# Grouped attention on one core: loads in order of need, a TensorE kept awake at the start, correction chains of eight with one step on GpSimd

## The chip, the cores and the metric

The kernel runs on one core of a Trainium2 chip. The metric is the device time of one execution in microseconds (us). Every time below is the median of a kernel's runs. In the profile PE is TensorE (its matmuls), PEld its weight loads, ACT ScalarE, DVE VectorE, POOL GpSimd, and SP or SPq is SyncE.

## The reference

```python
# q: 8 x 8 x 1024 x 64 (batch, query heads, sequence, head size); k, v: 8 x 2 x 1024 x 64; float32
scale = 1.0 / np.sqrt(head_dim)
for g in range(n_kv_heads):              # four query heads share one K and one V
    scores = scale * np.matmul(q_group, k_group.transpose(0, 1, 3, 2))
    attn = np.exp(scores - np.max(scores, axis=-1, keepdims=True))
    attn = attn / (np.sum(attn, axis=-1, keepdims=True) + 1e-08)
    output[:, q_start:q_end] = np.matmul(attn, v_group)
```

That is 64 heads. The kernel splits a head into two jobs of 512 queries and a job into eight blocks of 128 keys, so there are 128 jobs and 1024 blocks of scores of 128x512.

## The kernel before

Each block of scores needs an exponential, and two engines make them. ScalarE takes two blocks at a time from PSUM (128x1024). VectorE takes single blocks: it writes the bits of an approximate power of two, gathers four such blocks into a group, and corrects the group by a chain of four steps: an AND, a linear factor, a product, and an addition to the bits. (The plan and the prediction count the last two alike, as products: both are operations of two inputs, and they take the same time.) A plan, made before the launch from assumed durations, decides which block goes to which engine, and places every instruction in a fixed order.

```python
GROUP = 4
# in the plan: all four steps of a chain are VectorE's
CHAIN = (0.73, 0.73, 1.26, 1.26)
...
# one cursor `nxt` walks through all blocks; each goes to the engine that is free first
ta, td = ...            # when ScalarE's, when VectorE's PSUM bank is free
t, to_d = (ta, 0) if ta <= td else (td, 1)
```

Inputs are loaded in three stages. GpSimd issues a transfer that casts a head to bf16 into scratch memory; SyncE issues transfers that transpose it into SBUF, 256 rows at a time; K's parts are then placed into a padded set by four more transfers that GpSimd issues. SyncE also issues the 128 outputs.

```python
PIECE = 256
def cast(key, src):
    dma = nc.gpsimd.dma_start(out=scr..., in_=src...)
    tc.add_manual_dep(dma.ins, last_score[0].name, SYNC, reason="pace")   # not before this score
def transpose(key, dst, n):
    rows = slice(n * PIECE, (n + 1) * PIECE)
    nc.sync.dma_start_transpose(out=dst[:, rows], in_=src[rows, :])
def place_k(b, g, side, parity):
    nc.gpsimd.dma_start(out=ksets[b % 2][...], in_=kT[(b, g)][...])
...
elif step == 1:                                   # the linear factor
    nc.vector.tensor_scalar(out=y, in0=z, scalar1=CURVE_A / 128.0, scalar2=CURVE_B,
                            op0=ALU.mult, op1=ALU.add)
elif step == 2:
    nc.vector.tensor_tensor(out=y, in0=z, in1=y, op=ALU.mult)
...
def normalise(s):                                 # output bank -> SBUF -> memory
    nc.vector.reciprocal(out=rec, in_=o[:, :, D])
    nc.vector.tensor_tensor(out=ost, in0=o[:, :, 0:D], in1=rec..., op=ALU.mult)
    nc.sync.dma_start(out=out[b, h]..., in_=ost)
...
# when the loads stand in the queues, relative to a head's first score at th (plan time)
at(th - 28.0, cast, ("q", b, h), q[b, h])
at(th - 17.0 + n, transpose_q, b, h, n)           # n = 0, 1
at(th - 38.0, cast, ("k", b, g), k[b, g])
at(th - 27.0 + n, transpose_k, b, g, n)
at(th - 20.0, place_k, b, g, side, parity)        # four of them
```

Every engine works through its instructions in the order in which they were placed. This order is what the change edits.

The softmax here doesn't subtract the row's maximum and nothing guards it: scores larger than these inputs give would overflow.

Of the kernel before, what the change touches and what calls it, by code (L numbers as in the profile page):

```python
# [14 lines left out]
GROUP = 4  # L15


def make_plan(nj, nkc):
# [6 lines left out]
    QK, PV, EXP, P1, NORM = 0.214, 0.143, 0.925, 0.605, 0.57  # L25
    CHAIN = (0.73, 0.73, 1.26, 1.26)
    FROM_PE, FROM_ACT, FROM_DVE = 0.28, 0.18, 0.12
    LIVE_A, LIVE_D, PENDING, ONLY_A = 26, 6, 8, 14
    INF = 1e9
    n = nj * nkc  # L30
# [3 lines left out]
    nxt = 0  # L34
    open_jobs, next_job, rem, obank = [], 0, {}, {}
    open_a = None
# [5 lines left out]

    def first_free(slots):
        return min(range(len(slots)), key=lambda s: slots[s])

    while normed < nj:
        best = None
        if nxt < n:
            ta = td = INF
            if open_a is not None:  # L50
                ta = max(pe, open_a["t"])
            elif live["A"] < LIVE_A:
                ta = max(pe, min(a_free))
            if pending < PENDING and nxt < n - ONLY_A and (cur or live["D"] < LIVE_D):
                td = max(pe, min(bank))
            t, to_d = (ta, 0) if ta <= td else (td, 1)
            if t < INF:
                best = min(best or (INF,), (t, 1 + to_d, "qk", to_d))
        for i, s in enumerate(open_jobs):
            for c in rem[s]:  # L60
                at = max(pe, ready.get(s * nkc + c, INF))
                if at < INF:
                    best = min(best or (INF,), (at, 3 + i, "pv", (s, c)))
        if len(open_jobs) < 2 and next_job < nj:
            at = max(pe, min(obank_free), min(ready.get(next_job * nkc + c, INF) for c in range(nkc)))
            if at < INF:
                best = min(best or (INF,), (at, 3 + len(open_jobs), "open", next_job))
        for q, p, kind in ((normq, 0, "norm"), (p1q, 1, "p1"), (chainq, 2, "chain")):
            if q:
                best = min(best or (INF,), (max(dve, q[0][0]), p, kind, 0))  # L70
        if cur and nxt >= n - ONLY_A and not p1q:
            best = min(best or (INF,), (dve, 9, "flush", 0))
        t, _, kind, arg = best
        if kind == "qk":
            cell = nxt
            nxt += 1
            pe = t + QK
            if not arg:
                if open_a is None:
                    slot = first_free(a_free)  # L80
                    a_id += 1
                    live["A"] += 1
                    open_a = {"slot": slot, "t": a_free[slot], "cells": []}
                    a_free[slot] = INF
                o = open_a
                ops.append((t, "qk", cell, "A", a_id, o["slot"], len(o["cells"])))
                o["cells"].append(cell)
                home[cell] = ("A", a_id)
                if len(o["cells"]) == 2 or nxt >= n:
                    act = max(act, pe + FROM_PE)  # L90
                    ops.append((act, "exp", a_id, tuple(o["cells"])))
                    act += EXP * len(o["cells"]) / 2
                    a_free[o["slot"]] = act + FROM_ACT
                    uses[("A", a_id)] = len(o["cells"])
                    for x in o["cells"]:
                        ready[x] = act + FROM_ACT
                    open_a = None
            else:
                k = first_free(bank)
                bank[k] = INF  # L100
                pending += 1
                ops.append((t, "qk", cell, "D", k, 0, 0))
                p1q.append((pe + FROM_PE, cell, k))
# [28 lines left out]
        elif kind == "p1":  # L132
            _, cell, k = p1q.pop(0)
            if not cur:
                d_id += 1
                live["D"] += 1
            ops.append((t, "p1", cell, k, d_id, len(cur)))
            dve = t + P1
            bank[k] = dve + FROM_DVE
            cur.append(cell)  # L140
            home[cell] = ("D", d_id)
            if len(cur) == GROUP:
                chainq.append((dve, d_id, cur, 0))
                cur = []
        elif kind == "flush":
            chainq.append((dve, d_id, cur, 0))
            cur = []
        else:
            _, g, cells, step = chainq.pop(0)
            ops.append((t, "chain", g, len(cells), step))  # L150
            dve = t + CHAIN[step] * len(cells) / GROUP
            if step + 1 < len(CHAIN):
                chainq.insert(0, (dve, g, cells, step + 1))
            else:
                pending -= len(cells)
                uses[("D", g)] = len(cells)
                for x in cells:
                    ready[x] = dve + FROM_DVE
# [4 lines left out]
def kernel(  # L163
# [27 lines left out]
    PIECE = 256  # L191
    scale = 1.0 / math.sqrt(D)
# [15 lines left out]
    qT_pool = ctx.enter_context(tc.tile_pool(name="qTpool", bufs=8))  # L208
    kT_pool = ctx.enter_context(tc.tile_pool(name="kTpool", bufs=4))
    pa_pool = ctx.enter_context(tc.tile_pool(name="papool", bufs=26))  # L210
    pd_pool = ctx.enter_context(tc.tile_pool(name="pdpool", bufs=6))
# [13 lines left out]

    ident = const_pool.tile([128, 128], BF16)
    make_identity(nc, ident)
    vsets, ksets = [], []
    for s in range(2):
# [4 lines left out]
        for side in range(2):  # L234
            if s == 0:
                nc.vector.memset(ks[(1 - side) * D : (2 - side) * D, :, side, :], 0.0)
# [52 lines left out]
    def first_loads():  # L289

        staged = []
        for eng, src in ((nc.sync, k[0, 0]), (nc.scalar, q[0, 0])):
            f = first_pool.tile([128, NHC, 2, D], FP32, name=f"f{len(staged)}")
            eng.dma_start(
                out=f, in_=src.rearrange("(c p two) d -> p c two d", p=128, two=2)
            )
            staged.append(f)
        vf = first_pool.tile([128, NHC, 2, D], FP32, name="vf")
        nc.sync.dma_start(
            out=vf, in_=v[0, 0].rearrange("(c p two) d -> p c two d", p=128, two=2)  # L300
        )
        cast(("q", 0, 1), q[0, 1])
# [5 lines left out]
        for side in range(2):  # L308
            nc.gpsimd.memset(ksets[1][(1 - side) * D : (2 - side) * D, :, side, :], 0.0)  # L309
        fk, fq = staged  # L310

        hk = first_pool.tile([128, NHC, 3, D], BF16, name="hk")
        nc.vector.tensor_copy(out=hk[:, :, 0:2, :], in_=fk)  # L313
        nc.vector.tensor_copy(out=hk[:, :, 2, :], in_=fk[:, :, 0, :])
        hq = first_pool.tile([128, NHC, 2 * D], BF16, name="hq")
        nc.scalar.copy(out=hq, in_=fq.rearrange("p c two d -> p c (two d)"))
        tk = dbanks[0].tile([128, 2, HALF], BF16, name="dps0")
        tq = dbanks[1].tile([128, HALF], BF16, name="dps1")
        for w in range(2):
            for c in range(NHC):  # L320
                nc.tensor.transpose(  # L321
                    tk[:, w, c * 128 : (c + 1) * 128],
                    hk[:, c, w : w + 2, :].rearrange("p w d -> p (w d)"),
                    ident,
                )
        for c in range(NHC):
            nc.tensor.transpose(tq[:, c * 128 : (c + 1) * 128], hq[:, c, :], ident)
        qT[(0, 0)] = qT_pool.tile([128, HALF], BF16, name="qT")
        lo, hi = slice(0, D), slice(D, 2 * D)
        nc.vector.tensor_copy(out=ksets[0][lo, 0, 0, 0:HALF], in_=tk[lo, 0, :])  # L330
        nc.scalar.copy(out=qT[(0, 0)], in_=tq)
        nc.vector.tensor_copy(out=ksets[0][lo, 0, 0, HALF:S], in_=tk[lo, 1, :])
        nc.vector.tensor_copy(out=ksets[0][hi, 0, 1, 0:HALF], in_=tk[hi, 1, :])
        nc.vector.tensor_copy(out=ksets[0][hi, 0, 1, HALF:S], in_=tk[hi, 0, :])
# [46 lines left out]
    def exp_curve(g, m, step):  # L381
# [7 lines left out]
        elif step == 1:  # L389
            y = tmp_pool.tile([128, GROUP, QBS], FP16, name="y")[:, 0:m]  # L390
            temps[g].append(y)
            nc.vector.tensor_scalar(  # L392
# [56 lines left out]
    for op in plan:  # L449
        if op[1] == "qk":  # L450
            first_use.setdefault(op[2] // NKC, op[0])
        at(op[0], run[op[1]], *op[2:])
    for b in range(B):
        for h in range(H):
            if b == 0 and h == 0:
                continue
            th = first_use[(b * H + h) * 2]
            if (b, h) != (0, 1):
                at(th - 28.0, cast, ("q", b, h), q[b, h])
            for n in range(HALF // PIECE):  # L460
                at(th - 17.0 + n, transpose_q, b, h, n)
            if h % HPG == 0:
                g = h // HPG
                at(th - 38.0, cast, ("k", b, g), k[b, g])
                at(th - 33.0, cast, ("v", b, g), v[b, g])
                for n in range(HALF // PIECE):
                    at(th - 27.0 + n, transpose_k, b, g, n)
                for side in range(2):
                    for parity in range(2):
                        at(th - 20.0, place_k, b, g, side, parity)  # L470
                at(th - 15.0, place_v, b, g)
# [34 lines left out]
```

## Time and profile before

| | before |
|---|---|
| time, median of 3 runs | 397.44 us (397.31 to 398.06) |
| span of the profiled run | 395.58 us |
| first exponential starts | 8.16 us |
| exponentials on ScalarE | 412, busy 379.0 us |
| ScalarE idle between the first and the last | 1.05 us |
| end of the last to the end of the span | 7.38 us |
| VectorE busy; GpSimd busy | 375.8 us; 86.6 us |

The main views are shown in the prediction. The page cuts the span into 40 slices and gives each engine's busy tenths in each; these are ScalarE's and GpSimd's rows for the kernel before:

```profile
ACT  4999999999999999999999999999999999999992
POOL 5340303132041313113131040312214131120000
```

A 9 means 90% or more of the slice. ScalarE has no gap that shows at this scale, and GpSimd is mostly idle.

### The profile page before, as it was taken

The numbers are of one execution on the slowest core, as the hardware profiler recorded it, in microseconds if no ns is written. First come the engines' busy times: TensorE is split into PE (matmuls) and PEld (weight loads), VectorE is DVE, ScalarE is ACT, GpSimd is POOL, SyncE is SP. The second block draws the span as 40 slices with busy tenths as digits, with TensorE's granted clock in tenths as the row PEclk, the third lists the DMA queues.
The fourth block names the chain that finished last, engine by engine and source line by source line (L and its number), as shares of the span: only waits on it lengthen the run. The fifth ranks groups of instructions, "written<-read, shape, count | busy, mean of one in ns | idle before, by whom it ended". The sixth has DMA issues, their size and how long they took to land.

```text
span 395.6 us, 12683 instructions
## 1 busy us (share of the span) xinstructions
PE 365.7 (92%) x5043; PEld 233.0 (59%) x5132; DVE 375.8 (95%) x664; ACT 381.5 (96%) x415; POOL 86.6 (22%) x165
## 2 busy tenths in 40 slices
PE   4899999999999999999999999999999999999986
PEld 2455566565656556655656565565655666565655
DVE  4999999999999999999999999999999999999995
ACT  4999999999999999999999999999999999999992
POOL 5340303132041313113131040312214131120000
PEclk9999999999999999999999999999999999999999
DMA  4665866749676786847758686785965867574314
GB/s 106 106 125 111 163 107 127 128 86 160 103 139 130 132 143 101 142 90 145 115 103 141 111 141 112 118 143 98 155 109 115 149 132 121 99 130 99 68 28 94
DMA packets 134890, 46.72 MB, mean 118 GB/s; under 512 B 130848, under 2 KB 132384, under 8 KB 133344
## 3 DMA queue, kind: packets, MB, share of 16 engines
q1 hardware_dynamic: 129408, 29.52, 38.3%
q0 software_dynamic: 4896, 16.13, 27.0%
q8 instruction: 40, 0.66, 0.8%
q10 hardware_dynamic: 528, 0.26, 0.2%
q14 instruction: 18, 0.15, 0.2%
HBM read 27.13 MB, written 28.97 MB: 142 GB/s over the span
## 4 chain that ended last, share of the span: by engine, by line
ACT 67%; DVE 11%; PE 10%; issue 6%; DMA 3%; POOL 1%; SPq 0%
ACT pa L362 67%; PE ops L414 5%; PE aps L351 5%; DVE pd L371 3%; DVE y L402 2%; DVE pd L406 2%; DVE ost L429 1%; DMA vf<-in_v_dram 1%; PE dps L351 1%; DVE y L392 1%; DMA qT<-scr_q 1%; POOL kset L309 1%; DVE z L386 1%; DVE rec L427 1%; DMA scr_q<-in_q_dram 1%
## 5 line engine op out<-in xcount | busy, mean ns | idle before, releaser
L362 ACT ACTIVATE pa<-aps 128x1024 bf16<-128x1024 f32 x412 | 379.0, 1064 | 2.1 <-PE aps L351 1.3
L351 PE MATMUL aps<-qT,kset 128*128 128x512 bf16 x735 | 226.2, 379 | 15.5 <-ACT pa L362 13.6
L414 PEld LDWEIGHTS <-pa 128*128 128x128 bf16 x3296 | 134.5, 97 | 57.6 <-DVE ost L429 0.8
L414 PE MATMUL ops<-vset,pa 128*128 128x65 bf16 x3296 | 143.9, 193 | 3.4
L371 DVE TENSOR_SCALAR pd<-dps 128x512 uint16<-128x512 f32 x200 | 129.8, 682 | 2.2 <-PE dps L351 2.2
L351 PEld LDWEIGHTS <-kset 128*128 128x128 bf16 x1024 | 85.3, 97 | 66.3 <-issue 30.9
L248 POOL DMA_DIRECT2D scr_q<-in_q_dram x63 | 34.0, 540 | 173.4 <-PE aps L351 150.6
L351 PE MATMUL dps<-qT,kset 128*128 128x512 bf16 x200 | 64.5, 380 | 1.0
L406 DVE TENSOR_TENSOR pd<-pd,y 128x2048 uint16<-128x2048 uint16 x50 | 61.2, 1225 | 1.7
L402 DVE TENSOR_TENSOR y<-z,y 128x2048 f16<-128x2048 uint16 x50 | 61.2, 1225 | 1.7
L429 DVE TENSOR_TENSOR ost<-ops,rec 128x256 f32<-128x256 f32 x128 | 54.3, 425 | 4.4
L414 PEld LDWEIGHTS <-pd 128*128 128x128 bf16 x800 | 38.5, 97 | 29.8 <-DVE pd L406 7.9
L268 POOL DMA_DIRECT2D kset<-kT x60 | 32.2, 545 | 76.7 <-DMA kT<-scr_k 68.7
L414 PE MATMUL ops<-vset,pd 128*128 128x65 bf16 x800 | 45.3, 194 | 1.2
L392 DVE TENSOR_SCALAR y<-z 128x2048 f16<-128x2048 uint16 x50 | 34.3, 687 | 0.6
L386 DVE TENSOR_SCALAR z<-pd 128x2048 uint16<-128x2048 uint16 x50 | 34.2, 684 | 0.0
L427 DVE RECIPROCAL rec<-ops 128x4 f32<-128x4 f32 x128 | 22.6, 176 | 2.4 <-PE ops L414 1.9
L248 POOL DMA_DIRECT2D scr_v<-in_v_dram x15 | 7.6, 505 | 8.2 <-PE aps L351 7.1
L248 POOL DMA_DIRECT2D scr_k<-in_k_dram x15 | 8.1, 542 | 4.7 <-PE aps L351 4.3
L321 PE MATMUL dps<-ident,hk 128*128 128x128 bf16 x8 | 1.0, 311 | 5.0 <-DVE hk L313 5.0
L321 PEld LDWEIGHTS <-hk 128*128 128x128 bf16 x8 | 0.8, 141 | 5.0 <-DVE hk L313 5.0
L309 POOL MEMSET kset<- 64x2048 bf16 x2 | 3.6, 1798 | 0.1
(20 smaller groups left out, 9.7 us busy)
## 6 DMA issues: line engine op xcount, KB each, us to landing
out_dram<-ost SPq DMA_DIRECT2D x128, 128.0 KB, 3.2
scr_q<-in_q_dram POOLq DMA_DIRECT2D x63, 128.0 KB, 3.5
kset<-kT POOLq DMA_DIRECT2D x60, 64.0 KB, 2.7
qT<-scr_q SPq DMA_TRANSPOSE x126, 3.6
scr_k<-in_k_dram POOLq DMA_DIRECT2D x15, 128.0 KB, 4.2
scr_v<-in_v_dram POOLq DMA_DIRECT2D x15, 128.0 KB, 3.9
vset<-scr_v SPq DMA_DIRECT2D x30, 64.0 KB, 3.8
kT<-scr_k SPq DMA_TRANSPOSE x30, 3.4
```

The lines of the kernel that those rows point to most:

```text
L248: dma = nc.gpsimd.dma_start(out=scr.rearrange("(p f) -> p f", f=1024), in_=src.rearrange("(p s) d -> p (s d)", s=1024 // D),)
L268: nc.gpsimd.dma_start(out=ksets[b % 2][side * D : (side + 1) * D, g, side, parity * HALF : (parity + 1) * HALF], in_=kT[(b, g)][parity * D ...
L351: last_score[0] = nc.tensor.matmul(dst, lhsT=ksets[b % 2][:, h // HPG, side, c * 128 : (c + 1) * 128], rhs=qT[(b, h)], start=True, stop=Tr ...
L362: nc.scalar.activation(out=pt[:, 0:m], in_=psum.pop(("A", n))[:, 0:m], func=AF.Exp, scale=scale)
L371: nc.vector.tensor_scalar(out=groups[g][:, slot], in0=psum.pop(cell), scalar1=bits_scale, scalar2=bits_bias, op0=ALU.mult, op1=ALU.add,)
L386: nc.vector.tensor_scalar(out=z, in0=pd, scalar1=0x7F, scalar2=None, op0=ALU.bitwise_and)
L392: nc.vector.tensor_scalar(out=y, in0=temps[g][0], scalar1=CURVE_A / 128.0, scalar2=CURVE_B, op0=ALU.mult, op1=ALU.add,)
L402: nc.vector.tensor_tensor(out=y, in0=z, in1=y, op=ALU.mult)
L406: nc.vector.tensor_tensor(out=pd, in0=pd, in1=y, op=ALU.add)
L414: nc.tensor.matmul(ops_of[s][:, qs, :], lhsT=p_of[cell][:, qs * 128 : (qs + 1) * 128], rhs=vsets[b % 2][:, h // HPG, c, :], start=opens an ...
L427: nc.vector.reciprocal(out=rec, in_=o[:, :, D])
L429: nc.vector.tensor_tensor(out=ost, in0=o[:, :, 0:D], in1=rec.unsqueeze(2).to_broadcast([128, NQS, D]), op=ALU.mult,)
```

## The change

The intent has three parts. The linear factor of the chain goes to GpSimd, which has time to spare, and groups grow from four blocks to eight, so that fixed costs per instruction fall and VectorE gets slack. The plan lets VectorE work up to six jobs ahead of ScalarE, so that its blocks are ready early; the loads are issued by when they are needed, tighter at the start and wider later. At the start, Q and K are loaded in halves and TensorE runs blank products to leave its slow clock.

```diff
-GROUP = 4
+GROUP = 8
+POOL_STEP = 1
...
-    CHAIN = (0.73, 0.73, 1.26, 1.26)
-    LIVE_A, LIVE_D, PENDING, ONLY_A = 26, 6, 8, 14
+    EXP, AND, LINE, PRODUCT = (0.065, 0.4265), (0.20, 0.133), (0.25, 0.43), (0.16, 0.27)
+    CHAIN = (AND, LINE, PRODUCT, PRODUCT)
+    LIVE_A, LIVE_D, PENDING, PER_JOB, LEAD, RAMP, AHEAD, FIRST_PV = 28, 5, 16, 2, 6, 3, 0.08, 2.0
...
+        lead = min(LEAD, job_a // RAMP)
+        job_d = max(job_d, job_a + lead)          # VectorE's blocks are taken from this job on
...
         for side in range(2):
-            if s == 0:
-                nc.vector.memset(ks[...], 0.0)    # second set: on GpSimd, later
+            nc.vector.memset(ks[...], 0.0)        # both sets on VectorE
...
+        last_score[0] = keep_warm(WARM)           # 26 products of a blank tile
...
         elif step == 1:
-            nc.vector.tensor_scalar(
+            nc.gpsimd.tensor_scalar(
                 out=y, in0=temps[g][0], scalar1=CURVE_A / 128.0, ...
...
-            th = first_use[(b * H + h) * 2]
-                at(th - 28.0, cast, ("q", b, h), q[b, h])
-                at(th - 17.0 + n, transpose_q, b, h, n)
+            th = first_use[b * H + h]             # now VectorE's block, up to six jobs earlier
+            spare = min(1.0, max(0.0, th - 10.0) / 50.0)
+                casts.append((th - 12.0 - 14.0 * spare, ("q", b, h), q[b, h]))
+                at(th - 7.0 - 10.0 * spare + n, transpose_q, b, h, n)
...
-                at(th - 38.0, cast, ("k", b, g), k[b, g])
-                    at(th - 27.0 + n, transpose_k, b, g, n)
-                        at(th - 20.0, place_k, b, g, side, parity)
+                casts.append((th - 17.0 - 20.0 * spare, ("k", b, g), k[b, g]))
+                    at(th - 12.0 - 14.0 * spare + n, transpose_k, b, g, n)
+                        at(th - 6.0 - 9.0 * spare, place_k, b, g, side, parity)
```

The halves of the first Q and K, the spacing of the casts and some pool sizes are cut.

## The prediction

> **What bounds the kernel now.** I read the page's busy times first, then the waits, then the windows, then the timeline of the first 10 us and of the last 8.
>
> The busy times alone do not decide, since three engines are above 90%:
>
> ```profile
> PE 365.7 (92%) x5043; PEld 233.0 (59%) x5132; DVE 375.8 (95%) x664; ACT 381.5 (96%) x415; POOL 86.6 (22%) x165
> ...
> ACT 67%; DVE 11%; PE 10%; issue 6%; DMA 3%; POOL 1%; SPq 0%
> ```
>
> The second line is the chain that ended last. Two thirds of it is ScalarE, nearly all of it the exponentials. The groups of instructions show how little ScalarE ever waits between two of them (the last column is the idle time before the group):
>
> ```profile
> L362 ACT ACTIVATE pa<-aps 128x1024 bf16<-128x1024 f32 x412 | 379.0, 1064 | 2.1 <-PE aps L351 1.3
> ...
> L371 DVE TENSOR_SCALAR pd<-dps 128x512 uint16<-128x512 f32 x200 | 129.8, 682 | 2.2 <-PE dps L351 2.2
> ...
> L402 DVE TENSOR_TENSOR y<-z,y 128x2048 f16<-128x2048 uint16 x50 | 61.2, 1225 | 1.7
> ...
> L392 DVE TENSOR_SCALAR y<-z 128x2048 f16<-128x2048 uint16 x50 | 34.3, 687 | 0.6
> ```
>
> So 412 exponentials take 379.0 us, 0.920 us each (the 1064 ns of one overlap the next one). The windows split the span at the first exponential and at the end of the last:
>
> ```profile
> core 0: us, PE busy (x) PEld busy (x) DVE busy (x) ACT busy (x) POOL busy (x), PEclk, DMA share, GB/s
> 0.00:8.16 8.16, 2.51 (x15) 1.71 (x16) 3.97 (x8) 2.48 (x3) 3.66 (x12) 1.00 0.47 121
> ...
> 388.22:395.60 7.38, 3.46 (x106) 3.21 (x104) 2.80 (x9) 0.00 (x0) 0.00 (x0) 0.96 0.44 91
> ```
>
> The whole span is therefore 8.16 us before ScalarE starts, 380.06 us in which it hardly stops, and 7.38 us after it. **Time falls only by fewer exponentials, an earlier first one, or a shorter tail.** The measured time, 397.44 us, is 1.86 us above the profiled span of 395.58; I add this again at the end.
>
> VectorE is second. It computes the other exponentials (200 blocks of 128x512, by bit arithmetic and a correction chain) and normalises. TensorE's own load is less than its 365.7 us suggest: in the trace successive scores start 215 ns apart and successive output products 29 to 35 ns, so 1024 scores and 4096 products need about 220 + 125 = 345 us.
>
> **What the Trainium skill says.** "TensorE: Matmul & The Clock Gate", What's actually happening: the array is at half rate until it has been busy for some 3.4 us. The timeline agrees: the first four scores of 512 columns take 1.86 us from 7.11 us on (about 0.43 us apart), later ones 215 ns, although the clock row shows 9 throughout.
>
> "GPSIMD Engine Reference", Engine selection: GpSimd is about level with VectorE's plain rate for an operation of one input. The trace before has no such operation on GpSimd; its memset of 2048 bf16 took 1.80 us, or 0.88 ns an element. Estimate: 4096 elements take 3.6 us, against 1.2 us on VectorE, which gains from its fast modes.
>
> "SBUF — State Buffer", Who interferes with whom: a VectorE tensor_tensor with both inputs in SBUF holds up a GpSimd operation that reads SBUF, and the converse; so do VectorE's two-port modes. No run yet shows it here. VectorE's order of instructions speaks against trouble: between the AND of a group and its product, which waits for GpSimd, stand only bit conversions and normalisations, whose large input is in PSUM.
>
> **The change part by part.**
>
> ScalarE: the static order of instructions has 408 exponentials of 128x1024 against 412. 4 x 0.92 = **3.7 us less** on the bounding engine. This is the only lasting relief of the steady stage.
>
> VectorE, by durations of the groups: the linear factor leaves, -34.3 us. Three chain operations shrink from 50 of 2048 elements to 26 of 4096. A product took 1225 ns for 2048; at two elements a cycle of 0.96 GHz ("VectorE: DVE Perf Modes", Side-by-side) 1067 ns is data and 158 fixed, so 2.29 us for 4096 (an estimate); the AND likewise 1.22 us. 26 x (1.22 + 2 x 2.29) = 150.8 us against 34.2 + 2 x 61.2 = 156.6: -5.8. Eight more conversions, 8 x 0.65 = +5.2. Two more zero fills of 0.91 us, +1.8. Together about **-33 us, to some 343 us**. But VectorE hands only 8 more blocks back to itself, so most of this becomes idle time, worth nothing directly; it does make VectorE less likely to delay TensorE.
>
> GpSimd: 26 x 3.6 = +94 us of work, and two memsets of 1.8 us fewer: from 87 to about 177 us, less than half the span.
>
> TensorE: the same 1024 scores and 4096 products, 28 blank products at the start; no lasting change.
>
> Start: before, K lands at 4.47 and Q at 4.91, the transposes run from 4.98, the first score at 7.11, the first exponential at 8.16. After, VectorE has four zero fills ahead of its first K cast: from 1.02, a blank fill of about 0.1, 4 x 0.91 and a gap of 0.25 as before, so the cast starts at about 5.05, though the first half of K should land earlier. Two casts of 0.29 end at 5.6; the transposes that follow at 5.95; the copies back at 6.5. In TensorE's order four more transposes of K stand ahead of the first score, and they need a third cast (0.29): 6.85, then 7.25. Two scores warm are 0.43 and the handover 0.19: first exponential at about **7.9**. Against 8.16 that is -0.3: the fills and the third cast take back most of what halves and a warm clock give. The second and third exponentials need not wait for cold scores (before, their starts were 1.04 and 1.16 us apart rather than 0.92): -0.4.
>
> Tail: before, when the last exponential ended, TensorE still had 96 products to do (its last batch starts at 388.68 and ends at 391.82, after waiting for VectorE's chain). After, 16 products depend on the last exponential's tile and 56 more stand between the last score and them, of which most run while the last two exponentials do. Estimate: TensorE ends 1.0 us after the last exponential, the reciprocal and product take 0.6 us and a handover 0.2, then from issue of the output (392.52) to the span's end it was 3.1 us. 1.0 + 0.2 + 0.6 + 0.2 + 3.1 = 5.1 against 7.38: -2.2 us.
>
> Sum: -3.7 - 0.3 - 0.4 - 2.2 = -6.6. 397.44 - 6.6 = 390.8. VectorE's slack and loads issued earlier should save some of the small stalls (eight gaps of 1.14 to 1.24 us between exponentials, 2 us of excess in all); I take -0.4 net of new ones: **390.4 us**.
>
> **Rivals.** First, GpSimd's queue becomes the wait. The linear factor stands in one in-order queue with the casts, which wait for scores (150.6 us of idle time), and the placing of K, which waits for its transposes:
>
> ```profile
> POOL scr_q L248 <- PE aps L351: 150.6, 36, 5.9
> POOL kset L268 <- DMA kT<-scr_k: 68.7, 14, 8.6
> ...
> PE aps L351 <- ACT pa L362: 13.6, 44, 0.6
> ```
>
> A factor behind an 8.6 us wait would hold VectorE's product, the normalisations behind it, then the two output banks and TensorE. Against it: K's transposes are issued 11 us ahead of the placing instead of 7, the correction groups run six jobs ahead, and VectorE has some 1.7 us of slack per group ((388 - 343) / 26). If it bites in half of the 26 groups for 1 us each, the time is 395 to 403.
>
> Second, the early loads bind. Head 1 is needed by the sixth conversion, about 10.5 us, and landed at 9.79 before; the next at about 15, and its cast now precedes the GpSimd work that held it until 10.37. A miss costs 1 to 3 us once, 392 to 394.
>
> Third, everything works better than summed: the tail near 4.5 us, the first exponential near 7.2, and stalls gone so that pitches fall to the 0.904 us that a third of them show. That makes 386 to 388.
>
> **Range and chances.** The certain part is -3.7, the likely tail brings it to -6, and over 2% needs a time under 389.6, 0.8 below my estimate. With an error of some 3 us either way I give 386.6 to 394.6, and 0.39 for faster by over 2%, 0.58 for within, 0.03 for slower.
>
> **What would show it.** 408 exponentials with 0.92 us each, about 375 us busy; first at 7.9; 5.1 us from the last one's end to the span's; VectorE near 343 us; the factor near 3.6 us on GpSimd; VectorE waiting for GpSimd less than 20 us in total and ScalarE less than 3 us for scores. The prediction is wrong if ScalarE waits over 5 us in the middle, if products on VectorE last beyond 2.3 us because of GpSimd, or if the start is later than before.

## The result, and the profile after

The changed kernel is correct and takes **409.39 us** (four runs, 407.48 to 411.87), against 397.38 us (397.27 to 398.06) for the kernel before in the same rounds. The ratio is 1.030, with a 95% interval of 1.024 to 1.036: slower. Ratios here are the mean time of one kernel's fast runs over that of the other's fast runs of the same rounds, so they are not quite the ratio of the medians.

These are the same rows of the page for the changed kernel, with the granted clock of TensorE between them:

```profile
ACT  3999989979999499999989999999999989999995
POOL 3458536246506166264445627434553614620330
PEclk9999999999999699999999999999999999999999
```

ScalarE now has holes: small ones in the first quarter, a deep one (4) in slice 14, which is 132 to 142 us. TensorE's clock fell to 6 in the slice that holds it. The busy times, the chain that ended last and three groups of instructions, also from the page:

```profile
PE 365.8 (90%) x5070; PEld 233.7 (58%) x5160; DVE 348.5 (86%) x555; ACT 379.4 (94%) x413; POOL 179.6 (44%) x189
...
ACT 41%; PE 17%; issue 13%; DVE 12%; POOL 10%; DMA 5%; SPq 2%; POOLq 0%
...
L419 ACT ACTIVATE pa<-aps 128x1024 bf16<-128x1024 f32 x408 | 376.7, 1061 | 16.8 <-PE aps L408 13.4
...
L449 POOL TENSOR_SCALAR y<-z 128x4096 f16<-128x4096 uint16 x26 | 94.1, 3619 | 31.8 <-DVE z L443 20.3
...
L459 DVE TENSOR_TENSOR y<-z,y 128x4096 f16<-128x4096 uint16 x26 | 59.5, 2290 | 22.5 <-POOL y L449 22.5
```

ScalarE carried 67% of the chain before and carries 41% now; GpSimd, 1% before, has 10%. Of the engines that the page counts, none is busier than ScalarE, and ScalarE is less busy than before. So none of them has become the bound by its amount of work; SyncE's issuing is not counted there. The exponentials wait 16.8 us in all instead of 2.1, nearly all for scores. Of the windows, split again at the first exponential and the end of the last, the middle one (columns as in the prediction: stretch, length, then busy time of PE, PEld, DVE, ACT and POOL, clock, DMA share, GB/s):

```profile
9.12:401.24 392.12, 359.29 (x5008) 228.47 (x5097) 341.86 (x541) 376.70 (x408) 176.58 (x177) 0.99 0.66 115
```

The span grew by 10.12 us. Its parts: the start is 0.95 us later (9.116 against 8.163), the exponentials take 2.3 us less (376.7 against 379.0), ScalarE's idle time between them is 15.4 us (392.12 - 376.70) against 1.05, so 14.4 more, and the tail is 2.9 us shorter (405.70 - 401.24 = 4.46 against 7.38). The gains that were predicted are there; the loss is in the middle. The waits say for what (engine, instruction and line, what it waited for, then us in total, times, longest):

```profile
ACT pa L419 <- PE aps L408: 13.4, 12, 4.7
...
POOL kset L299 <- DMA kT<-scr_k: 12.9, 4, 7.1
...
PE ops L471 <- DVE ost L486: 8.2, 6, 4.1
...
PE dps L408 <- DMA qT<-scr_q: 3.5, 4, 1.2
```

Two stories can be read in these lines, and the timeline shows both.

**Theory A: GpSimd's queue.** This is the timeline around the deepest hole (start, duration, engine and line, operation; in brackets the idle time before it and what ended it):

```profile
120.58 11.17 ACT L419 ACTIVATE pa<-aps 128x1024 bf16<-128x1024 f32 x12
...
120.72 2.25 SPq L291 DMA_TRANSPOSE kT<-scr_k  x1
...
121.32 1.22 DVE L443 TENSOR_SCALAR z<-pd 128x4096 uint16<-128x4096 uint16 x1
...
125.77 2.09 POOL L299 DMA_DIRECT2D kset<-kT  x4 [3.14 <-DMA kT<-scr_k]
...
127.87 3.64 POOL L449 TENSOR_SCALAR y<-z 128x4096 f16<-128x4096 uint16 x1
...
131.54 2.29 DVE L459 TENSOR_TENSOR y<-z,y 128x4096 f16<-128x4096 uint16 x1 [5.02 <-POOL y L449]
...
133.96 0.42 DVE L486 TENSOR_TENSOR ost<-ops,rec 128x256 f32<-128x256 f32 x1
...
134.44 1.04 PE L471 MATMUL ops<-vset,pa 128*128 128x65 bf16 x16 [4.10 <-DVE ost L486]
135.29 1.04 PE L408 MATMUL aps<-qT,kset 128*128 128x512 bf16 x2
...
136.43 1.02 ACT L419 ACTIVATE pa<-aps 128x1024 bf16<-128x1024 f32 x1 [4.68 <-PE aps L408]
```

Read it downwards. VectorE's AND (z) ends at 122.54, and the factor could start. But four placings of K stand ahead of it in GpSimd's queue, and they wait 3.14 us for K's transpose, which SyncE issued only at 120.72. The placings take 2.09 us more; the factor starts at 127.87, 5.3 us late. VectorE stands still for 5.02 us in front of its product, although a normalisation stands behind it whose matmuls had ended by 129 us. The normalisation frees an output bank; TensorE waits 4.10 us for it and, in its own order, cannot start the next scores; ScalarE waits 4.68 us for those. After the pause scores start 0.43 us apart instead of 0.215, and ScalarE idles another 1.1 us. The window view shows half the clock granted at just this time (columns as above):

```profile
132.51:139.34 6.83, 4.90 (x43) 2.96 (x43) 6.22 (x9) 2.05 (x2) 0.49 (x1) 0.50 0.86 150
```

"TensorE: Matmul & The Clock Gate", What's actually happening, states that an idle window of about 3.4 us brings the half clock back. The trace agrees that idle time brings it back, but less was enough here: in the 3.41 us before (129.10 to 132.51) TensorE was still busy for 1.24 us. The same page, in Architectural detail, says that VectorE, ScalarE and GpSimd are strict FIFOs; the 5.02 us in front of ready work agree with that too.

Four of the 26 factors start more than 2 us after their AND has ended, each behind placings of K: those whose AND ends at 76.1, 122.5, 200.6 and 317.3 us, late by 5.1, 5.3, 2.2 and 3.0 us. VectorE's product waits 3.2, 5.0, 2.75 and 3.5 us there, 14.5 of its 22.5 us. I traced ScalarE's stalls behind these four one by one; they add up to about 13 us, of which 11.9 are idle time (2.7, 5.8, 1.3 and 2.0 us), and the rest is overlap: an exponential after a stall overlaps none before it, which costs some 0.14 us (1.064 - 0.920) each time.

**Theory D: loads come late because SyncE's queue is behind.** This is the timeline of the changed kernel some 80 us earlier:

```profile
42.34 1.23 SPq L291 DMA_TRANSPOSE qT<-scr_q  x1
43.66 1.20 SPq L492 DMA_DIRECT2D out_dram<-ost  x2
44.91 2.08 SPq L291 DMA_TRANSPOSE qT<-scr_q  x1
47.09 3.25 SPq L291 DMA_TRANSPOSE kT<-scr_k  x2
...
50.16 0.60 PE L408 MATMUL dps<-qT,kset 128*128 128x512 bf16 x2 [0.83 <-DMA qT<-scr_q]
...
51.29 1.02 ACT L419 ACTIVATE pa<-aps 128x1024 bf16<-128x1024 f32 x1 [0.73 <-PE aps L408]
```

SyncE goes from one issue to the next without a pause. The two transposes of head 9 are issued at 42.3 and 44.9 us, the data lands at 50.1, and the score that needs it starts at 50.1 after waiting. The plan had them in SyncE's queue 13 and 12 us ahead of that score (7 + 10 * spare, the second 1 us later). Eight heads land less than 0.5 us before their first score, all between 20 and 81 us (before, one in the whole kernel), and the four stalls that follow cost ScalarE 3.7 us, 3.2 of them idle time. With theory A's 11.9 that is 15.1 of the 15.4 us of idle time, so the two leave little room for a third cause. The reason for this stretch is the ramp: the lead of VectorE's blocks grows by one job for every three, so three extra heads are asked for in the first 60 us.

K is late for the same reason. From the issue of K's first transpose to the first placing the plan has 11 us, from the last one 10; the trace has 5.0 us from the last one in the median. (In the kernel before, the plan had 7 and 6, the trace 3.5.)

How full SyncE's queue is can only be bounded. Its records of issuing cover 91% of the time from 20 to 360 us (before: 94%). A record can contain waiting, and taking out what the trace calls waiting leaves about 64% (before: 63%). A transpose's record is not mostly waiting: 104 of the 156 contain no wait that the trace tells, and these too last 1.23 us in the median. SyncE's waits for VectorE's results show, further down, on which side of the work it runs.

### The profile page after: what moved, and what is told of

Same layout as the page of the kernel before. It is cut to its first block, busy times and chain, and to the rows that moved or that the text cites. A ratio compares the mean times of both kernels' runs of the same rounds, so it can differ in the third digit from the quotient of the medians.

```text
span 405.7 us, 12626 instructions
## 1 busy us (share of the span) xinstructions
PE 365.8 (90%) x5070; PEld 233.7 (58%) x5160; DVE 348.5 (86%) x555; ACT 379.4 (94%) x413; POOL 179.6 (44%) x189
## 4 chain that ended last, share of the span: by engine, by line
ACT 41%; PE 17%; issue 13%; DVE 12%; POOL 10%; DMA 5%; SPq 2%; POOLq 0%
ACT pa L419 41%; PE aps L408 7%; POOL y L449 7%; PE ops L471 6%; DVE pd L463 4%; PE dps L408 3%; DVE pd L428 2%; DMA qT<-scr_q 2%; POOL kset L299 2%; DVE ost L486 2%; SPq L291 2%; DMA kT<-scr_k 2%; POOL scr_q L279 1%; DVE rec L484 1%; DVE kset L267 1%
## 5 line engine op out<-in xcount | busy, mean ns | idle before, releaser
L419 ACT ACTIVATE pa<-aps 128x1024 bf16<-128x1024 f32 x408 | 376.7, 1061 | 16.8 <-PE aps L408 13.4
L471 PE MATMUL ops<-vset,pa 128*128 128x65 bf16 x3264 | 148.6, 194 | 10.3 <-DVE ost L486 7.8
L428 DVE TENSOR_SCALAR pd<-dps 128x512 uint16<-128x512 f32 x208 | 135.0, 683 | 9.5 <-PE dps L408 8.5
L449 POOL TENSOR_SCALAR y<-z 128x4096 f16<-128x4096 uint16 x26 | 94.1, 3619 | 31.8 <-DVE z L443 20.3
L279 POOL DMA_DIRECT2D scr_q<-in_q_dram x63 | 38.2, 606 | 138.4 <-PE aps L408 71.8
L459 DVE TENSOR_TENSOR y<-z,y 128x4096 f16<-128x4096 uint16 x26 | 59.5, 2290 | 22.5 <-POOL y L449 22.5
L408 PE MATMUL dps<-qT,kset 128*128 128x512 bf16 x208 | 72.8, 379 | 5.4 <-DMA qT<-scr_q 3.5
L463 DVE TENSOR_TENSOR pd<-pd,y 128x4096 uint16<-128x4096 uint16 x26 | 59.4, 2284 | 0.2
L299 POOL DMA_DIRECT2D kset<-kT x60 | 31.5, 544 | 17.6 <-DMA kT<-scr_k 12.9
L443 DVE TENSOR_SCALAR z<-pd 128x4096 uint16<-128x4096 uint16 x26 | 31.7, 1218 | 0.0
L267 DVE MEMSET kset<- 64x1024 uint32 x4 | 3.6, 912 | 1.0 <-issue 1.0
L339 PE MATMUL ops<-blank 128*128 128x128 bf16 x28 | 3.4, 313 | 1.0 <-DVE blank L257 1.0
```

Of the source, the lines that this page charges most:

```text
L279: dma = nc.gpsimd.dma_start(out=scr.rearrange("(p f) -> p f", f=1024), in_=src.rearrange("(p s) d -> p (s d)", s=1024 // D),)
L299: nc.gpsimd.dma_start(out=ksets[b % 2][side * D : (side + 1) * D, g, side, parity * HALF : (parity + 1) * HALF], in_=kT[(b, g)][parity * D ...
L408: last_score[0] = nc.tensor.matmul(dst, lhsT=ksets[b % 2][:, h // HPG, side, c * 128 : (c + 1) * 128], rhs=qT[(b, h)], start=True, stop=Tr ...
L419: nc.scalar.activation(out=pt[:, 0:m], in_=psum.pop(("A", n))[:, 0:m], func=AF.Exp, scale=scale)
L428: nc.vector.tensor_scalar(out=groups[g][:, slot], in0=psum.pop(cell), scalar1=bits_scale, scalar2=bits_bias, op0=ALU.mult, op1=ALU.add,)
L443: nc.vector.tensor_scalar(out=z, in0=pd, scalar1=0x7F, scalar2=None, op0=ALU.bitwise_and)
```

## The experiments

Sixteen kernels were run, each next to the kernel before on the same chip, whose median was 397.5 to 398.1 us. All gave correct results. Edits are against the changed kernel unless it is said otherwise. Where an expectation names a theory by a letter, A and D are those above; any other rival is described where it is named. "Idle" is ScalarE's idle time between its first and last exponential in the profiled run (15.4 us in the changed kernel, 1.05 before), and "late heads" are those whose Q landed less than 0.5 us before its first score.

### 1. Placings of K go behind a factor that is near (klate)

```diff
+    factors = [o[0] for o in plan if o[1] == "chain" and o[4] == POOL_STEP]
+    def behind(t):                    # due less than 4 us ahead of a factor: just after it
+        return min([f + 0.001 for f in factors if t <= f < t + 4.0] or [t])
-                        at(th - 6.0 - 9.0 * spare, place_k, b, g, side, parity)
+                        at(behind(th - 6.0 - 9.0 * spare), place_k, b, g, side, parity)
```

> One edit: a placing of K that the plan has less than 4 us ahead of a linear factor goes behind it in GpSimd's queue. Theory A (the linear factor waits behind the placing of K in GpSimd's in-order queue; VectorE's product, then the normalisation, an output bank, TensorE and ScalarE wait in turn): of the four late groups in the changed kernel (late by 5.1, 5.3, 2.2 and 3.0 us) this edit moves the last three and not the first, so VectorE's wait for GpSimd falls from 22.5 to about 11 us, and the time by about 10 us (what the stalls of those three cost ScalarE), to about 399. Rival B (chains of eight as such: operations of 2.3 us hold up the normalisations) and rival C (GpSimd and VectorE block each other at SBUF): order does not matter, 407 to 412.

Measured: 409.03 us, ratio 1.0295 (1.027 to 1.032). A miss. The waits of this run:

```profile
POOL kset L299 <- DMA kT<-scr_k: 32.9, 7, 8.3
...
DVE y L459 <- POOL y L449: 21.9, 17, 5.1
```

The factor at 122 us was cured, yet GpSimd now waits 32.9 us for K instead of 12.9, and four factors, three of them others than before, are 2.1 to 6.2 us late. The order in the plan kept the placing away from the factor by plan time, but K arrived later still, and the placing held the next factor. Order alone does not repair it while K comes late.

### 2. K is placed by SyncE (ksp)

```diff
-        nc.gpsimd.dma_start(        # in place_k
+        nc.sync.dma_start(
```

> One edit: the placing of K is issued by SyncE instead of GpSimd; the order on TensorE, VectorE and ScalarE is the same. Theory A: no linear factor is over 1.5 us late, VectorE waits for GpSimd 8 us or less in total, and the time falls by about 13 us, to 395 to 398, unless SyncE, blocked by its own wait for K's transposes, delays Q instead (then waits for qT grow beyond the 5 us of the changed kernel). Rivals B and C: 407 to 412.

Measured: 453.16 us (452.60 without the slow run), ratio 1.132 (one of its four runs, 454.69, was slow and is left out of the ratio).

In the waits, VectorE's for the factor fall from 22.5 to 6.7 us, as theory A expects once nothing blocks GpSimd. But 60 more transfers on SyncE make the rest of its queue late: 30 of 63 heads are late, and TensorE's wait for Q in front of VectorE's scores rises from 3.5 to 40.6 us. This was the first sign that SyncE had no room.

### 3. The factor back on VectorE, order unchanged (factor_vec)

```diff
-            nc.gpsimd.tensor_scalar(    # step 1
+            nc.vector.tensor_scalar(
```

> One edit: the linear factor runs on VectorE, with the same plan and the same chains of eight. Theory A: no wait for GpSimd can arise; VectorE's busy time grows by 26 x 1.2 = 32 us to about 380, ScalarE's idle time falls to 3 to 8 us, and the time is 396 to 401. Rival B (chains of eight as such): the stalls stay, 405 or more. Rival C (blocking at SBUF): like A here.

Measured: 409.67 us (405.98 to 411.76), ratio 1.029. Idle is still 13.0 us. The wait for the factor is gone, but the plan believes VectorE to be free while it computes the factor, and TensorE then waits 10.3 us for VectorE's PSUM banks. Theory A's 396 to 401 was missed. Two effects are mixed, so the run tells nothing apart.

### 4. The same with the plan made anew (replan_vec)

```diff
-POOL_STEP = 1
+POOL_STEP = -1
-    CHAIN = (AND, LINE, PRODUCT, PRODUCT)
+    CHAIN = (AND, AND, PRODUCT, PRODUCT)
-            nc.gpsimd.tensor_scalar(
+            nc.vector.tensor_scalar(
```

> The linear factor on VectorE, and the plan told so: 411 exponentials instead of 408, 202 blocks on VectorE. Theory A: 411 x 0.922 = 379 us of exponentials, start and tail as in the changed kernel (9.1 and 4.5 us or a little more) and 4 to 6 us of stalls from late Q: 396 to 401. Rival B: above 405.

Measured: 405.49 us (403.08 to 407.93), ratio 1.0195 (1.015 to 1.024), with 411 exponentials on ScalarE. GpSimd's step is gone entirely, and the kernel is still some 8 us slower than before; idle is 12.8 us, 18 heads are late, and TensorE waits 8.7 us for Q. So theory A is not the whole cause: without any factor on GpSimd the idle time is nearly as long, and Q is late. By the number alone, runs 3 and 4 came out as rival B of the expectations had it (chains of eight as such, 405 or more). That rival falls with runs 10, 11 and 14: they keep the chains of eight, and their idle time is 0.6 to 1.0 us.

### 5. A slower ramp of the lead (lead6_8)

```diff
-    ... LEAD, RAMP ... = ... 6, 3, ...
+    ... LEAD, RAMP ... = ... 6, 8, ...    # one job of lead per eight jobs, not three
```

> One number: VectorE's lead over ScalarE grows by one job in 8 instead of 3 (to the same 6 jobs). 408 exponentials as in the changed kernel. Theory D (SyncE's queue issues transposes and outputs 90 to 93% of the time in both kernels, so the three extra heads of Q that the lead asks for in the first 60 us come late, and K with them): the margin between the landing of a head of Q and its first score, under 0.5 us for 8 heads in the changed kernel, is over 1 us for all or nearly all, and ScalarE's stalls on Q (3.7 us) fall under 1 us; the late linear factor at 80 us goes too if K is on time; the time falls to 399 to 405, the rest being linear factors behind the placing of K (theory A). Against D: Q stalls stay as they are.

Measured: 405.63 us (405.34 to 409.93), ratio 1.024. TensorE no longer waits for Q (one late head, median margin 6.8 us). The gain of some 3.8 us is as much as the Q stalls cost in the changed kernel's trace (3.7), but the intervals of the two ratios overlap (1.018 to 1.0295 here), so the size is not certain. The waits that remain are theory A's: VectorE's for the factor are 24.1 us, GpSimd's for K 17.8.

### 6. Slower ramp and placings behind factors (lead6_8_klate)

Edits 1 and 5 together.

> The slower lead, and a placing of K less than 4 us ahead of a linear factor goes behind it. A and D together: VectorE waits for GpSimd under 10 us in total, ScalarE idles under 6 us, 395 to 400. If K's placing alone (4 issues of 0.54 us) still meets the factors, or K is late again, 400 to 406.

Measured: 406.01 us (405.81 without the slow run), ratio 1.021 (1.019 to 1.022; one run of 411.64 was slow and is left out of it). A miss again: VectorE still waits 20.3 us for the factor, GpSimd 32.7 us for K, and ten heads are late. The wait moved.

### 7. Factor on VectorE with a new plan, slower ramp (rv_lead6_8)

Edits 4 and 5 together.

> Linear factor on VectorE, plan told so, and the slower lead: 411 exponentials as in the run with the faster lead (405.5 us, whose stalls the trace puts down to late Q). D: Q's margins recover, stalls under 5 us, 396 to 400. Against D: 403 to 408 again.

Measured: 403.55 us (401.21 to 404.25), ratio 1.014 (1.011 to 1.017). Idle is 10.2 us, 15 heads are late and TensorE waits 9.9 us for Q. That is the outcome which the expectation put down against D: the ramp is not what makes Q late here. Q is late all the same, with the slow ramp and no factor on GpSimd, so either SyncE's queue is behind even then, which runs 10 and 11 test, or D is wrong. This kernel is the base of two runs below.

### 8. No lead at all (lead0_3)

```diff
-    ... LEAD, RAMP ... = ... 6, 3, ...
+    ... LEAD, RAMP ... = ... 0, 3, ...
```

> No lead at all: VectorE takes its blocks from the job that ScalarE works on or the next, as before the change; linear factor on GpSimd, chains of eight. The plan has 399 exponentials. D: Q's margins as in the kernel before (median near 6.7 us), no Q stalls. 399 x 0.923 = 368 us busy, and with 9.1 before and 5 after, 2 for the launch and 10 to 15 us of stalls from late factors (A, less hidden because a block is needed sooner): 394 to 401. If GpSimd's lateness is harmless, 385 to 389.

Measured: 429.78 us, ratio 1.079, far outside the expected range. Q is no longer the trouble (two late heads, median margin 10.3 us), but VectorE's blocks are now needed too soon after they are begun: TensorE waits 18.6 us for the end of a chain, idle is 28.8 us and the tail 21.4. The lead is a needed part of chains of eight; it cannot simply be dropped to spare the loads.

### 9. Slower ramp, placings behind factors, K asked for 8 us earlier (kearly)

Edits 1 and 5, and:

```diff
-   casts.append((th - 17.0 - 20.0 * spare, ("k", b, g), k[b, g]))
+   casts.append((th - 17.0 - 28.0 * spare, ("k", b, g), k[b, g]))
-       at(th - 12.0 - 14.0 * spare + n, transpose_k, b, g, n)
+       at(th - 12.0 - 22.0 * spare + n, transpose_k, b, g, n)
```

> The slower lead, each placing of K behind a factor that is less than 4 us later, and K cast and transposed 8 us earlier, so that the placing seldom blocks GpSimd on a transpose. Theory A: VectorE waits for GpSimd under 10 us (24 with the slower lead alone), ScalarE's idle time falls from 14 to under 7 us, 396 to 401. If the wait for GpSimd falls and the time does not, something else takes its place: theory D says Q (late because SyncE issues without a pause).

Measured: 408.89 us, ratio 1.028, outside the expected 396 to 401.

```profile
DVE y L459 <- POOL y L449: 11.1, 14, 2.2
PE dps L408 <- DMA qT<-scr_q: 10.6, 6, 4.6
```

With K early the factor's waits fall from 24.1 (run 5) to 11.1 us. In exchange Q is late: 13 heads, 10.6 us. K and Q share SyncE's queue, and what one gains by an earlier place the other loses. Runs 1, 2, 6 and 9 each mended one wait and raised another; what is left to test is the queue itself.

### 10 and 11. Relief for SyncE, twice, with the factor on VectorE (rv_lead6_8_outpool, rv_lead6_8_piece512)

Both start from run 7. The first takes the outputs out of SyncE's queue; the second halves the number of transposes, with the same rows moved.

```diff
-        nc.sync.dma_start(          # run 10: the 128 outputs
+        nc.gpsimd.dma_start(
```

```diff
-    PIECE = 256                     # run 11: two transposes of 256 rows per head ...
+    PIECE = 512                     # ... become one of 512
```

> Linear factor on VectorE, slower lead, and the 128 outputs issued by GpSimd, which has room, instead of SyncE. Theory D (SyncE's issuing is full, so Q is late): SyncE's issuing falls from about 92% to some 75% of the time, Q's margin returns to over 4 us in the median and its stalls (about 10 us of ScalarE's time in the run with outputs on SyncE) fall under 2 us: 403.5 - 9 = 393 to 397, which would be as fast as the kernel before or faster. Against D: Q as late as before, 401 to 405; or the casts, now behind outputs in GpSimd's queue, make Q late in another way.

> The same relief by another means: one transpose of 512 rows instead of two of 256, outputs on SyncE. D: if one issue of 512 rows takes SyncE less than two of 256 (1.2 to 1.6 us each now), Q's stalls shrink and the time falls below 400; if it takes twice as long, 402 to 405 as without it. Tells whether SyncE's time goes by instruction or by row.

Measured: 394.25 us, ratio 0.9905 (0.989 to 0.992), and 393.38 us, ratio 0.989 (0.987 to 0.9905), against 1.014 for run 7. Idle falls from 10.2 to 0.7 and 1.0 us, and TensorE waits 0.9 and 0 us for Q instead of 9.9. This is the wait in run 7 and then in run 10; run 11 has no such line:

```profile
PE dps L408 <- DMA qT<-scr_q: 9.9, 10, 2.6
```

```profile
PE dps L408 <- DMA qT<-scr_q: 0.9, 1, 0.9
```

Two different reliefs give the same gain of some 10 us. They share only that SyncE's queue is shorter: run 10 changes nothing in the transposes, run 11 nothing in where outputs are issued. Theory D is shown for this base.

### 12. The second set's fills back on GpSimd (fills_pool)

```diff
-            nc.vector.memset(ks[...], 0.0)
+            if s == 0:
+                nc.vector.memset(ks[...], 0.0)
...
+        for side in range(2):                     # after V's two copies
+            nc.gpsimd.memset(ksets[1][...], 0.0)
```

> The changed kernel with the two zero fills of the second K set back on GpSimd. The first K cast starts when K has landed, near 4.3 us instead of 5.5, and the first exponential about 1.0 us earlier than in the changed kernel (9.1, or 8.1 to 8.5 in the runs in which TensorE's clock happened to be up): 7.2 to 8.2. The rest as in the changed kernel, 406 to 411.

Measured, one look only: 410.19 us, a single run of unknown state, so the time is no verdict. The start is what the run was for. VectorE's timeline at the start of the changed kernel:

```profile
4.69 0.91 DVE L267 MEMSET kset<- 64x1024 uint32 x1 [0.25 <-issue]
5.53 0.42 DVE L368 CAST hk<-fk 128x256 bf16<-128x256 f32 x2
```

and the same cast in this run:

```profile
3.64 0.29 DVE L369 CAST hk<-fk 128x256 bf16<-128x256 f32 x1 [0.35 <-DMA fk<-in_k_dram]
```

Without the two fills the first cast of K starts when the half of K lands, 1.9 us earlier, and the first exponential at 6.80 us instead of 9.12. Part of those 2.3 us is the cast and part a TensorE at full clock: in this run the first four scores take 1.03 us, in the changed kernel 1.83.

### 13. One transpose of 512 rows, nothing else (piece512)

```diff
-    PIECE = 256
+    PIECE = 512
```

> The changed kernel with one transpose of 512 rows instead of two of 256; same order on TensorE, VectorE and ScalarE. D says: no Q stalls (3.7 us in the changed kernel), SyncE issuing near 57% of the time, K on time, so that GpSimd waits for K's transposes hardly at all (12.9 us). What is left is the placing of K itself ahead of some factors, 4 issues or 2.2 us late at the most; a factor that was 2.2 us late cost ScalarE 1.6 us. 394 to 400. If the factors' lateness had nothing to do with SyncE: 404 to 408.

Measured: 397.19 us (396.84 to 399.1), ratio 0.9998 (0.995 to 1.004). One line takes back 12 us, three percent. A transpose's record on SyncE lasts 1.23 us in the median for 256 rows and 1.19 us for 512, so the total for transposes falls from 229 to 112 us. The data lands no sooner after an issue (4.0 us in the median for Q, 3.7 without the edit), so the gain is not a quicker transfer. SyncE's waits for VectorE to finish an output, in the changed kernel and then in this run:

```profile
SPq L492 <- DVE ost L486: 40.0, 34, 3.6
```

```profile
SPq L492 <- DVE ost L486: 129.4, 82, 4.6
```

Before the edit SyncE seldom had to wait for an output, because it reached it late; now it mostly stands ready before the output is. K's one transpose is issued 10.6 us ahead of the placing in the median (planned 11; 5.0 for the last of two without the edit), GpSimd never waits for K, and no head is late. What is left is in ScalarE's group and in VectorE's wait:

```profile
L419 ACT ACTIVATE pa<-aps 128x1024 bf16<-128x1024 f32 x408 | 376.1, 1065 | 6.6 <-PE aps L408 6.2
...
L459 DVE TENSOR_TENSOR y<-z,y 128x4096 f16<-128x4096 uint16 x26 | 59.5, 2289 | 17.0 <-POOL y L449 17.0
```

Three factors are still 2.2, 2.2 and 3.0 us late. They stand behind four placings of K, which now wait for nothing but take 0.54 us each to issue: pure order, theory A without theory D.

### 14. The same with placings behind factors (p512_klate)

Edits 13 and 1 together.

> The same, and each placing of K that has a factor less than 4 us behind it goes after that factor. A says that now, with K and Q on time, the order counts: VectorE waits for GpSimd under 9 us in total, ScalarE idles under 4 us: 388 to 394, 2 to 7 us below the run with the transposes alone. If the two are equal, the placing's own 2.2 us do no harm.

Measured: 392.52 us (391.94 to 393.16), ratio 0.987 (0.984 to 0.990). The edit that did nothing in run 1 is worth 4.7 us here.

```profile
ACT 75%; PE 10%; issue 6%; DVE 5%; POOL 2%; DMA 1%; ACTq 0%
...
L419 ACT ACTIVATE pa<-aps 128x1024 bf16<-128x1024 f32 x408 | 375.5, 1067 | 2.0 <-PE aps L408 1.6
```

No factor is more than 1.3 us late (VectorE still waits 10.6 us for it in total, a little over the expected 9), idle is 0.62 us, and ScalarE carries 75% of the chain, more than before the change.

### 15. With K earlier and the fills on GpSimd (p512_kearly_fills)

Edit 14, K earlier as in run 9, and edit 12.

> All repairs: 512-row transposes, K 8 us earlier and behind the factors, and the second K set's zero fills on GpSimd, which brought the first exponential from 9.1 to 6.8 us. 408 x 0.920 = 375.4, 6.8 before, 4.5 after, 2 of idle time, 1.9 for the launch: 388 to 392, faster than the kernel before by 1.5 to 2.5%.

Measured: 391.12 us (390.7 to 391.72), ratio 0.983 (0.980 to 0.9865). The first exponential starts at 7.41 us (with the first scores at the slow clock again: four take 1.91 us) and idle is 1.7 us. This is the fastest version found, 1.7% faster than the kernel before.

### 16. The relief alone, on the kernel before (before_p512)

The edit of run 13, applied to the kernel before.

> The kernel before with 512-row transposes. Its ScalarE idles about 1 us between the first and last exponential, so relieving SyncE can't give much: 396 to 398.

Measured: 397.54 us, ratio 0.9994 (0.996 to 1.0025). It is worth nothing there. Run 13's 12 us are thus no free gain of larger transposes; they are the part of the changed kernel's loss that came through SyncE.

## Why the prediction was wrong, point by point

The prediction said 390.4 us with a range up to 394.6 (4 us either way, not the 3 that it names, and neither reaches the result); the time was 409.39. Most terms of its sum were right. One step, which set a rival aside, was not.

| term | predicted | measured |
|---|---|---|
| exponentials on ScalarE | 408, 375 us | 408, 376.7 us; 375.5 once the stalls are gone (run 14) |
| factor on GpSimd | 3.6 us each | 3.62 us |
| product; AND on VectorE | 2.29; 1.22 us | 2.29; 1.22 us |
| VectorE; GpSimd busy | 343; 177 us | 348.5; 179.6 us |
| first exponential | 7.9 us | 9.12 us |
| last exponential to the end | 5.1 us | 4.46 us |
| new stalls in the middle | -0.4 us net | +14.4 us |

**The costs of the operations were right.** The fear of SBUF was rightly set aside for the factor: factors last 3.59 to 3.66 us and products 2.28 to 2.29. But the order of instructions spared them the test, since only conversions, reciprocals and normalisations ran beside a factor. GpSimd's other work was held up: 13 of the 63 casts of Q were issued beside an AND, and these took 1.02 us in the median, against 0.49 for the 27 beside neither an AND nor a product (in the kernel before, whose AND is half as long, 0.70 against 0.49). No term of the sum has this. What it cost was not tested. The 2.3 us instead of 3.7 that four exponentials fewer saved are explained by the overlap lost after stalls; with the stalls gone the same 408 save 3.5.

**The step that failed** is the dismissal of the first rival, "GpSimd's queue becomes the wait". Its chain of events, factor behind K's placing, product, normalisations, output banks, TensorE, was exactly what the trace shows. It was set aside with three arguments. "K's transposes are issued 11 us ahead of the placing instead of 7" is plan time: on the chip the last of them was 5.0 us ahead instead of 10, and already before the change 3.5 instead of 6. "The correction groups run six jobs ahead" does not help, because the wait does not reach TensorE through the group's own blocks; it reaches it through normalisations of other jobs that stand behind the product. "VectorE has some 1.7 us of slack per group" is a mean; the slack was met by four delays of 2.2 to 5.3 us, of which 1.3 to 5.8 us each came out at once as idle time of ScalarE. In its place the runs showed about 13 us of stalls behind those four factors. Even the rival's own size, 395 to 403, was too small.

**What was left out** is SyncE. No view in the prediction counts its issuing, and the page's busy times do not list it; only its line of 68.7 us in which GpSimd waits for K's transposes hinted at it. The plan asks it for Q and K earlier, while it was already behind its plan before the change. The second rival named late loads, but as one miss of 1 to 3 us at the start; it was eight late heads and 3.7 us of stalls until 81 us, and through late K it also fed the first rival.

The runs give these sizes. Relief of SyncE alone takes the changed kernel from 409.4 to 397.2 us (run 13), which is 12 us: the Q stalls, some 3.8 us of which run 5 took away by another route, and the placings' waits for K. Order alone is worth 4.7 us on top (run 14) and nothing without the relief (run 1). Together they leave 392.5 us, 2.1 above the 390.4 of the prediction's sum, of which the late start is 1.2. That late K feeds the first path also fits the failures of runs 1, 2, 6 and 9, which left as many issues on SyncE or added some.

**The start** was 1.2 us off. The gap of 0.25 us that the prediction counted once stands ahead of each of the four fills (they start 1.16 us apart), so K's first cast came at 5.53 instead of 5.05 us. And the warm clock was not there: 26 blank products occupied TensorE for some 2.9 us, then it idled 1.9 us until K's cast, and the first scores started 0.43 us apart, as cold as before. The first exponential varied between runs that have the same start, from 8.07 us (run 6, whose first three scores start 0.22 us apart) to 9.18 (run 9). The idle time is not the whole reason: runs 12 and 15 have the same start, with no idle time after the blank products, and the first four scores took 1.03 us in the one and 1.91 in the other. "TensorE: Matmul & The Clock Gate", What's actually happening, states that the window of about 3.4 us runs freely and that the warm-up so differs from run to run; these numbers agree with it, so a warm start was luck in the runs that had it; no run here tested a longer warm-up.

**Still open:** how much of SyncE's record of an issue is waiting (its share of the time lies between 64% and 91%), why some transposes last over 2 us, and how the 12 us of run 13 divide between Q and K.

## What to carry to other kernels

An engine with much idle time is not a free place for work on the critical chain: look at what stands in front of the new instruction in that engine's queue and how long the longest of it waits, since most of a delay is passed on through the in-order queues behind it (here 15.6 us of late factors became 11.9 us of idle time). A plan's lead in time is worth only what the issuing queue can keep, so compare planned and traced leads of the kernel before, and count the issues on SyncE as work of an engine. When single repairs only move a wait, look for the queue that the waits share; here one transpose in place of two, useless in the kernel before, turned a change that lost 3% into one that gains 1.3% with the order mended.

## What the Trainium skill lacked or had wrong

- "DMA: Bandwidth & Descriptors", Issuing engines are not separate DMA queues, says that issuing from several engines saves only the sequencer's time to initiate a transfer, "which is usually small relative to the DMA itself". Here it is not small: a transpose's record on SyncE lasts 1.23 us, also where the trace shows no wait in it, against 3.7 us from issue to landing, and taking 128 outputs off SyncE moved the ratio from 1.014 to 0.9905 (run 10).
- The same page gives no duration for issuing a DMA transpose of 256 or 512 rows on this chip; its one count per transpose instruction is for small tiles of earlier generations. The record lasts 1.23 us in the median for 256 rows and 1.19 us for 512 (run 13), so between these two sizes it goes by instruction and not by row.
- "GPSIMD Engine Reference", Engine selection, weighs an operation by its rate. The rate was right (3.62 us for 4096 elements), but the page, which names DMA issues among the engine's work, says nothing of what they cost an operation behind them in its queue: 0.54 us for each placing of K, and up to 7.1 us of waiting in front of one.
- "TensorE: Matmul & The Clock Gate", What's actually happening, gives an idle window of about 3.4 us as what brings the half clock back. Here it came back after 3.41 us in which TensorE was busy for 1.24 us, and in run 5 after such stretches with 0.87 and 1.58 us.
